# A feed-forward block on one core: ScalarE seeds the accumulation banks, and one more pair is computed by seven quarter products

## Chip, core and metric

The kernel runs on one core of a Trainium2 chip. The metric is device time in microseconds; the median of three runs is compared. Engines: PE is TensorE's matmul, PEld its weight load, DVE is VectorE, ACT is ScalarE, POOL is GpSimd, SP is SyncE, which here issues the weight DMAs.

## The reference

One residual block on x with 512 rows and 1024 columns, in float32:

```python
def _swiglu(x, w_in, w_out):
    gate, up = jnp.split(x @ w_in, 2, axis=-1)
    return (jax.nn.silu(gate) * up) @ w_out

h = x
h = h + 0.5 * _swiglu(_rmsnorm(h, ffn1_norm), ffn1_w_in, ffn1_w_out)
z = _rmsnorm(h, mix_norm) @ w_in
...                                   # conv module and gated linear attention on z
h = h + jnp.concatenate([y_conv, y_gla], axis=-1) @ w_out
h = h + 0.5 * _swiglu(_rmsnorm(h, ffn2_norm), ffn2_w_in, ffn2_w_out)
gate = jax.nn.sigmoid(_rmsnorm(h, ple_norm) @ ple_w_gate)
h = h + gate * (p @ ple_w_proj)
return _rmsnorm(h, final_norm)
```

The two SwiGLU layers have 2816 hidden columns (`ffn1_w_in` is 1024 x 5632, `ffn1_w_out` 2816 x 1024). "First layer" and "second layer" below are these two.

## The kernel before

**Matmuls in three parts.** Each float32 operand is split into a high part in the matmul's type and a low part (value minus high part). A product is three matmuls: high by high, high by low, low by high (`mm3`, and inside `mul`). For weights, ACT makes the high part (`high`, a cast), DVE the low part (`low`, a subtraction), 128 x 1024 elements at a time. The pools `raw` (fetched weights), `wh` and `wl` (parts) have six buffers each; `sm` (weight sums) has two.

**h.** The residual is kept transposed: eight tiles `hT[0..7]`, 128 columns of the model by 512 rows each.

**A layer** is written by `ffn`. The 22 blocks of 128 hidden columns are 11 pairs. A pair needs gate and up of two blocks, which is a 2 x 2 block product: weights a11, a12 (gate; first and second half of the model's columns) and a21, a22 (up), against the normalised input in four quarters b11, b12, b21, b22.

- *Plain pair:* eight half units h0 to h7 (`plain_unit`), each 12 matmuls on 512 columns. Units h0 to h3 give the gate of the two blocks, h4 to h7 the up; every second unit ends a bank.
- *Pair by seven quarter products* (Winograd's form of Strassen's scheme): units m1, m2, m6, m7, m5, m4, m3 (`mul`), each 24 matmuls on 256 columns, with weight operands a11, a12, s2, s3, s1, a22, s4. The sums s1 to s4 are made by DVE (`s12`, `s3_`, `s4_`, four operations on 128 x 1024), the input sums t1 to t4 once for the layer (`Right.split` makes their parts at given units, the hooks).

In a quarter-product pair, `p.x` is the bank that m1, m6, m5 and m3 add up in, `p.w` that of m7 and m4, `p.y` that of m2. ACT copies `p.x` to SBUF after m1 (`p.a`), m6 (`p.u2`) and m5, and DVE adds the copies to the other banks (`plus`). The first half of the gate is `p.a + p.y`, times the row factor, then silu (`gate0`).

**The output projection** takes the hidden blocks in five cuts, `CUTS = ((0, 4), (4, 8), (8, 12), (12, 16), (16, 22))`. `second` writes a cut as pieces: two of the eight blocks of h each, 24 matmuls on 512 columns in two banks. When a block's sum is complete, DVE does `h = 0.5 * ps + h`. The last cut's pieces are in two halves; the others are one piece each (`begin` and `final` both true).

**Order.** `ffn` lists the units, and each unit has jobs (fetch, weight sums, parts) that are written a given number of units ahead (`AHEAD` is 4). `drive` writes them out: a unit's jobs, then the first of the follow-ups left by the unit before, then the unit, then the other follow-ups. PE, DVE and ACT run exactly in the order written, since `Ordered` chains each one's instructions. SP's DMAs and POOL's instructions aren't chained. A tile takes any free buffer of its pool, and what first writes it waits for that buffer's last reader. PSUM has seven banks for these (`bank`).

In both layers, pair 0 is made before `ffn`, pairs 1 and 2 are plain (`plain` is `(1, 2)`) and pairs 3 to 10 by quarter products. From there an iteration i is m6, m7, m5 of pair i, m1 and m2 of pair i+1, a piece of an earlier cut, m4 and m3 of pair i, and another piece. In the last iteration pieces of the last cut stand in the gaps and after it. In the first layer, m4 of pair 10 also starts loading and splitting weights of the next stage (`ahead`).

Of the kernel before, what the change touches and what calls it, by code (L numbers as in the profile page):

```python
# [62 lines left out]
def block_kernel(ctx: ExitStack, tc: tile.TileContext, a: dict, out: bass.AP):  # L63
# [32 lines left out]
    def bank():  # L96
        return pp.tile([P, SEQ], F32, tag="mm", bufs=7, name=nm("ps"))
# [108 lines left out]

        return low(high(r3))

    def mm3(ps, wh, wl, xh, xl, first, last):
        pe.matmul(ps, wh, xh, start=first, stop=False)  # L210
        pe.matmul(ps, wh, xl, start=False, stop=False)
        pe.matmul(ps, wl, xh, start=False, stop=last)

    def ahead(src, c0, ncol):

# [71 lines left out]
    class Norm:  # L287
# [5 lines left out]
        def add(self, h):  # L293
            if self.n == 0:
                act.activation(self.acc, h, AF.Square)
            else:
                sq = tmp("sq", bufs=3)
                act.activation(sq, h, AF.Square)
                self.engine.tensor_tensor(out=self.acc, in0=self.acc, in1=sq, op=ALU.add)
            self.n += 1  # L300
# [8 lines left out]
    def mul(ps, w, x, first, last, ks=range(4)):  # L309

        (wh, wl), k0 = w, ks[0]
        for k in ks:
            xh, xl = x[k]
            for i in range(2):
                cs = slice(i * P, (i + 1) * P)
                o = ps[:, i * HALF:(i + 1) * HALF]
                end = last and k == ks[-1] and i == 1
                pe.matmul(o, wh[:, k - k0, cs], xh, start=(first and k == ks[0] and i == 0), stop=False, skip_group_check=True)
                pe.matmul(o, wh[:, k - k0, cs], xl, start=False, stop=False, skip_group_check=True)
                pe.matmul(o, wl[:, k - k0, cs], xh, start=False, stop=end, skip_group_check=True)  # L320
# [200 lines left out]
    mid = []  # L521
# [73 lines left out]
    def ffn(w_in, w_out, x, gname, given, first, rsb, hooks, plain):  # L595
# [17 lines left out]
        def silu(g):  # L613
            s = tmp("s")
            act.activation(s, g, AF.Silu)
            return s

        def plus(ps, t, i, name):
            o = tmp(name)
            dve.tensor_tensor(out=o, in0=ps, in1=t, op=ALU.add)  # L620
            dve.tensor_tensor(out=two(o), in0=two(o), in1=row(i), op=ALU.mult)
            return o

        def scaled(ps, name):
            o = tmp(name)
            dve.tensor_tensor(out=o, in0=ps, in1=got['rsb'], op=ALU.mult)
            return o
# [6 lines left out]
        def snap(ps, name, **kw):  # L634
            o = tmp(name, **kw)
            act.copy(o, ps)
            return o
# [11 lines left out]
        def m1(p):  # L649
            p.x = bank()  # L650
            mul(p.x, p.part("a11"), x.op["b11"], True, False)
            p.a = snap(p.x, "sq", bufs=3)

        def m2(p):
            p.y = bank()
            mul(p.y, p.part("a12"), x.op["b21"], True, True)

            def gate0():
                p.s0 = silu(plus(p.y, p.a, 0, "g1"))

            return [gate0]

        def m6(p):
            mul(p.x, p.part("s2"), x.op["t2"], False, False)
# [19 lines left out]
        def plain_unit(j):  # L684

            up, i, k = j // 4, j // 2 % 2, j % 2
            def run(p):
                if not j:
                    p.g, p.s = {}, {}
                if not k:  # L690
                    p.x = bank()
                ps = p.x
                wh, wl = p.part(f"a{1 + up}{1 + k}")
                cs = slice(i * P, (i + 1) * P)
                for c in range(4):
                    mm3(ps, wh[:, c, cs], wl[:, c, cs], *x.rows[4 * k + c], k == c == 0, k == 1 and c == 3)
                if not k:
                    return []
                if not up:
                    def gate():  # L700
                        p.s[i] = silu(scaled(ps, "g1"))
                    return [gate]
                return [lambda: gated_block(p, p.s[i], scaled(ps, "u1"), i),
                        lambda: act_parts(p) if i else None]
            return run
# [29 lines left out]
        def second(cut):  # L735

            f0, f1 = cut
            last = f1 == CUTS[-1][1]
            kn = f1 - f0
            nk = kn // 2 if last else kn  # L740
            ps = {}

            def piece(n, g, begin, final, key=None):

                def get():
                    got[f0, n, g] = load(w_out, f0 + g * nk, nk, n * P, 2 * P)

                def make():
                    got[f0, n, g] = parts(got[f0, n, g])

                def run():
                    left = []
                    wh, wl = got.pop((f0, n, g))
                    for i in range(2):
                        if begin:
                            ps[n + i] = bank()
                        cs = slice(i * P, (i + 1) * P)
                        for kk in range(nk):
                            k = g * nk + kk
                            f = f0 + k  # L760
                            mm3(ps[n + i], wh[:, kk, cs], wl[:, kk, cs], *pairs[f // 2].acts[f % 2],
                                k == 0, k == kn - 1)
                        if final:
                            h = hT[n + i]
                            dve.scalar_tensor_tensor(out=h, in0=ps[n + i], scalar=0.5, in1=h,
                                                     op0=ALU.mult, op1=ALU.add)
                            if last:
                                hi = bt(F32R, "hgH")
                                act.activation(hi, h, AF.Copy, scale=vec(gname, n + i))
                                left.append((h, hi, vec(gname, n + i)))  # L770
                    if key:
                        hooks.get(key, lambda *_: None)()
                    if not left:
                        return []

                    def lower():
                        for h, hi, g in left:
                            lo = bt(F32R, "hgL")
                            dve.scalar_tensor_tensor(out=lo, in0=h, scalar=g, in1=hi.bitcast(F32),
                                                     op0=ALU.mult, op1=ALU.subtract)  # L780
                            nhg.append((hi, lo))

                    lower()
                    for h, *_ in left:
                        norm.add(h)

                return [(7, get), (AHEAD, make)], run

            if not last:
                return [piece(n, 0, True, True, ("g2", f0) if n == 0 else None) for n in range(0, DC, 2)]  # L790
            return ([piece(n, 0, True, False) for n in range(0, 6, 2)],
                    [piece(n, 1, False, True) for n in range(0, 6, 2)] + [piece(6, 0, True, False),
                                                                           piece(6, 1, False, True)])

        units, had = [], set()

        def add(kind, i):
            if 0 <= i < npair and (kind, i) not in had:
                had.add((kind, i))
                units.append(unit(kind, i))  # L800
# [4 lines left out]
        for i in plain:  # L805
# [4 lines left out]
                    due = due[1:]  # L810
            if i in cut_of:
                due += second(cut_of[i])
        for unit_ in (("m1", start), ("m2", start), ("m1", start + 1)):
            add(*unit_)
        for i in range(start, npair):
            add("m6", i)
            add("m7", i)
            add("m5", i)
            if i == end:
                half, rest = second(cut_of[i])  # L820
                units.append(half[0])
            else:
                add("m1", i + 1)
            add("m2", i + 1)
            units += due[:1]
            add("m4", i)
            add("m3", i)
            units += due[1:2]
            due = due[2:]
            if i in cut_of and i < end:  # L830
                due += second(cut_of[i])
# [18 lines left out]
    def sums_hooks(x, names, at):  # L850

        h = {}
        for name, key in zip(names, at):
            h[key] = lambda *_, name=name: x.split(name)
        return h
# [569 lines left out]
    u1_ = plain_block(w0, 1, 1)  # L1425
    steps[3]()
    steps[4]()
    hooks = sums_hooks(xb, ("t2", "t3", "t1", "t4"), (("h7", 1), ("h2", 2), ("h5", 2), ("m1", 3)))
    hooks.update({("m7", 10): lambda *_: turn_p(0), ("m5", 10): lambda *_: turn_p(1)})
    hg, norm = ffn(ffn2_in, a["ffn2_w_out"][0], xb, "ple_norm", wf, ((g0, u0), (g1_, u1_)), lambda: mid[1], hooks, (1, 2))  # L1430
    in_order(False)
    pool.on = False
    rs = None
# [95 lines left out]
```

## Time and profile before

| | us |
|---|---|
| median of three runs | 965.26 |
| lowest and highest | 964.85, 966.62 |
| span of the profiled execution | 964.1 |
| first layer, quarter-product part and its end | 95 to 364 |
| mixer and its projections | 364 to 547 |
| second layer, plain part (pairs 0 to 2) | 547 to 631 |
| second layer, quarter-product part and its end | 631 to 897 |
| last gate, projection and norm | 897 to 964 |

The span runs from the first to the last instruction of one profiled execution. Its own time isn't told apart from the three runs; the median is 1.2 us above the span. Almost all instructions carry one line number, that of a recording helper (L46), so groups are told by tile names: `ps` is a bank; `wr`, `wh`, `wl` are fetched weights and their parts; `sm` weight sums; `hgH`, `hgL` parts of the normalised input; `t1H` and so on parts of its sums; `actH`, `actL` parts of the hidden blocks; `g` and `s` a gate before and after silu; `u` and `u2` the up side; `m` their product; `sq` a snapshot of a bank; `h` the residual; `wa` weights of the next stage.

In a group's row stand the engine, the operation, out<-in, the shapes and the count; after the bar its busy time in us, the mean of one in ns, and the idle time of the engine ahead of it with what ended it. In a row of waits stand total, number and longest. A row of the timeline starts with start and duration in us. In a row of windows stand the stretch, its length, and busy time and count of each engine.

### The profile page before, as it was taken

How to read it: one execution, taken by the hardware profiler on the slowest of the kernel's cores; microseconds unless marked ns; L12 is line 12 of the kernel's file. 1: busy time of each engine (PE TensorE's matmuls, PEld its weight loads, DVE VectorE, ACT ScalarE, POOL GpSimd, SP SyncE). 2: the span in 40 equal slices, each digit the busy share in tenths (PEclk: the TensorE clock that was granted, in tenths of full speed). 3: DMA queues.
4: the chain of work that ended last, by engine and by line, in shares of the span. 5: the costliest groups of instructions: out<-in, count | busy, mean ns of one | idle time of the engine just before them, and what ended most of it. 6: DMA issues, size and time to landing. Idle time of an engine off the chain costs nothing.

```text
span 964.1 us, 14124 instructions
## 1 busy us (share of the span) xinstructions
PE 949.9 (99%) x5737; PEld 837.3 (87%) x5737; DVE 736.7 (76%) x983; ACT 435.1 (45%) x661; POOL 39.7 (4%) x49
## 2 busy tenths in 40 slices
PE   8999999999999999999999999999999999999996
PEld 7888999999999978788877888899999999998885
DVE  4877787878788585999986676678978778867554
ACT  4753444344433453463564644354434434345442
POOL 0000000000000410001120000000000000000000
PEclk9999999999999999999999999999999999999999
DMA  8432323243223561125543234123343233334102
GB/s 250 142 117 67 106 74 124 92 132 102 74 88 119 145 173 48 41 85 134 132 100 99 79 96 129 46 67 113 105 132 109 68 106 113 109 110 153 45 1 88
DMA packets 102853, 99.14 MB, mean 103 GB/s; under 512 B 4499, under 2 KB 95717, under 8 KB 102788
## 3 DMA queue, kind: packets, MB, share of 16 engines
q1 hardware_dynamic: 100916, 94.05, 31.6%
q0 software_dynamic: 1296, 3.67, 2.2%
q8 instruction: 45, 0.74, 0.3%
q10 hardware_dynamic: 576, 0.52, 0.2%
q14 instruction: 20, 0.16, 0.1%
HBM read 92.46 MB, written 2.10 MB: 98 GB/s over the span
## 4 chain that ended last, share of the span: by engine, by line
PE 95%; DMA 1%; DVE 1%; ACT 1%; issue 1%; POOL 0%; SPq 0%; POOLq 0%; DVEq 0%; ACTq 0%
PE ps L46 94%; PE ax L46 1%; DMA wr<-in_w_in 1%; DMA x<-in_x 0%; DVE wl L46 0%; ACT wh L46 0%; POOL wa L46 0%; ACT wa L46 0%; DVE g L46 0%; ACT yc L46 0%; DVE ygL L46 0%; DVE actL L46 0%; DVE yc L46 0%; ACT ygH L46 0%; POOLq L1525 0%
## 5 line engine op out<-in xcount | busy, mean ns | idle before, releaser
L46 DVE TENSOR_TENSOR wl<-wr,wh 128x1024 fp32r<-128x1024 f32 (+2 forms) x180 | 213.2, 1196 | 53.5 <-ACT wh L46 53.3
L46 PE MATMUL ps<-hgH,wh 128*128 128x256 f32 (+1 forms) x768 | 243.3, 322 | 0.0
L46 PE MATMUL ps<-hgH,wl 128*128 128x256 f32 (+1 forms) x768 | 241.7, 320 | 0.0
L46 PE MATMUL ps<-hgL,wh 128*128 128x256 f32 (+1 forms) x768 | 241.1, 319 | 0.0
L46 ACT CAST wh<-wr 128x1024 fp32r<-128x1024 f32 (+2 forms) x185 | 186.2, 1022 | 57.9 <-PE ps L46 38.1
L46 PEld LDWEIGHTS ps<-hgH,wh 128*128 128x128 f32 x768 | 146.3, 191 | 13.0 <-ACT hgH L46 2.0
L46 PEld LDWEIGHTS ps<-hgL,wh 128*128 128x128 f32 x768 | 146.6, 191 | 10.7
L46 PEld LDWEIGHTS ps<-hgH,wl 128*128 128x128 f32 x768 | 145.9, 191 | 9.6
L46 PE MATMUL ps<-actH,wh 128*128 128x512 f32 x352 | 138.4, 393 | 1.3 <-ACT actH L46 1.3
L46 PE MATMUL ps<-actL,wh 128*128 128x512 f32 x352 | 138.1, 392 | 0.2 <-DVE actL L46 0.2
L46 PE MATMUL ps<-actH,wl 128*128 128x512 f32 x352 | 137.8, 391 | 0.0
L46 ACT ACTIVATE s<-g 128x512 f32<-128x512 f32 x48 | 30.4, 633 | 186.3 <-DVE g L46 186.2
L46 DVE SCALAR_TENSOR_TENSOR cv<-glu,cw,cv 128x504 f32<-128x504 f32 (+25 forms) x120 | 81.3, 731 | 0.6
L46 PEld LDWEIGHTS ps<-actH,wh 128*128 128x128 f32 x352 | 66.6, 189 | 14.7 <-ACT actH L46 1.7
L46 PEld LDWEIGHTS ps<-actH,wl 128*128 128x128 f32 x352 | 66.5, 189 | 14.1
L46 PEld LDWEIGHTS ps<-actL,wh 128*128 128x128 f32 x352 | 66.7, 189 | 13.2 <-DVE actL L46 0.5
L46 DVE SCALAR_TENSOR_TENSOR h<-ps,h 128x512 f32<-128x512 f32 x80 | 54.1, 687 | 30.8 <-PE ps L46 30.8
L46 PE MATMUL ps<-wh,hgH 128*128 128x512 f32 (+1 forms) x136 | 52.4, 385 | 0.0
L46 PE MATMUL ps<-wl,hgH 128*128 128x512 f32 (+1 forms) x136 | 51.8, 381 | 0.0
L46 PE MATMUL ps<-wh,hgL 128*128 128x512 f32 (+1 forms) x136 | 51.3, 377 | 0.0
L46 ACT COPY sq<-ps 128x512 f32<-128x512 f32 x32 | 18.7, 585 | 67.3 <-PE ps L46 67.3
L46 ACT CAST actH<-m 128x512 fp32r<-128x512 f32 x44 | 25.7, 618 | 46.1 <-DVE m L46 46.1
(226 smaller groups left out, 1564.7 us busy)
## 6 DMA issues: line engine op xcount, KB each, us to landing
wr<-in_ffn_w_in SPq DMA_DIRECT2D x84, 512.0 KB
wr<-in_ffn_w_out SPq DMA_DIRECT2D x32, 512.0 KB
wr<-in_w_in SPq DMA_DIRECT2D x20, 512.0 KB
wr<-in_ffn_w_out SPq DMA_DIRECT2D x16, 384.0 KB
wr<-in_w_out SPq DMA_DIRECT2D x8, 512.0 KB
wr<-in_ple_w_gate SPq DMA_DIRECT2D x8, 512.0 KB
wl<-wr POOLq DMA_DIRECT2D x5, 512.0 KB, 5.6
x<-in_x SPq DMA_DIRECT2D x8, 256.0 KB
```

Source lines behind the costliest of these rows:

```text
L46: inst = call(*args, **kwargs)
```

## The change

- For the first four cuts, ACT writes 2h into the two banks of a piece two units ahead of it (`seed`); the matmuls add to that without a start flag, and ACT writes 0.5 times the bank back to h. DVE's operation on h goes there. The last cut is as before.
- After m1, ACT copies `p.x` into a new bank `p.y` in place of an SBUF tile; m2 adds to it, and the gate is that bank times the row factor.
- The silu of a gate is written as a second follow-up, behind the next unit's matmuls.
- m1 of pair i+1 stands ahead of m5 of pair i; at the start m1 of the first two pairs stands ahead of m2.
- In the second layer pair 2 is made by quarter products (`plain` is `(1,)`), and the parts of the input sums are made earlier.

```diff
-    def mm3(ps, wh, wl, xh, xl, first, last):
+    def mm3(ps, wh, wl, xh, xl, first, last, skip=False):
...
         def m1(p):
             p.x = bank()
             mul(p.x, p.part("a11"), x.op["b11"], True, False)
-            p.a = snap(p.x, "sq", bufs=3)
+            p.y = bank()
+            act.copy(p.y, p.x)

         def m2(p):
-            p.y = bank()
-            mul(p.y, p.part("a12"), x.op["b21"], True, True)
+            mul(p.y, p.part("a12"), x.op["b21"], False, True)

             def gate0():
-                p.s0 = silu(plus(p.y, p.a, 0, "g1"))
-
-            return [gate0]
+                p.g0 = times_row(p.y, 0, "g1")
+
+            def gate1():
+                p.s0 = silu(p.g0)
+
+            return [gate0, gate1]
...
                 if not up:
                     def gate():
-                        p.s[i] = silu(scaled(ps, "g1"))
-                    return [gate]
+                        p.g[i] = scaled(ps, "g1")
+
+                    def gate1():
+                        p.s[i] = silu(p.g[i])
+
+                    return [gate, gate1]
...
+                onto = begin and final
+
+                def seed():
+                    for i in range(2):
+                        ps[n + i] = bank()
+                        act.activation(ps[n + i], hT[n + i], AF.Copy, scale=2.0)
...
-                        if begin:
+                        if begin and not onto:
                             ps[n + i] = bank()
...
                             mm3(ps[n + i], wh[:, kk, cs], wl[:, kk, cs], *pairs[f // 2].acts[f % 2],
-                                k == 0, k == kn - 1)
-                        if final:
+                                k == 0 and not onto, k == kn - 1, onto)
+                        if onto:
+                            act.activation(hT[n + i], ps[n + i], AF.Copy, scale=0.5)
+                        elif final:
...
-                return [(7, get), (AHEAD, make)], run
+                return [(7, get), (AHEAD, make)] + ([(2, seed)] if onto else []), run
...
-        for unit_ in (("m1", start), ("m2", start), ("m1", start + 1)):
+        for unit_ in (("m1", start), ("m1", start + 1), ("m2", start)):
             add(*unit_)
         for i in range(start, npair):
             add("m6", i)
             add("m7", i)
+            add("m1", i + 1)
             add("m5", i)
             if i == end:
                 half, rest = second(cut_of[i])
                 units.append(half[0])
-            else:
-                add("m1", i + 1)
             add("m2", i + 1)
...
-    hooks = sums_hooks(xb, ("t2", "t3", "t1", "t4"), (("h7", 1), ("h2", 2), ("h5", 2), ("m1", 3)))
+    hooks = sums_hooks(xb, ("t2", "t3", "t1", "t4"), (("h5", 1), ("h7", 1), ("m1", 2), ("m1", 3)))
...
-    hg, norm = ffn(ffn2_in, a["ffn2_w_out"][0], xb, "ple_norm", wf, ((g0, u0), (g1_, u1_)), lambda: mid[1], hooks, (1, 2))
+    hg, norm = ffn(ffn2_in, a["ffn2_w_out"][0], xb, "ple_norm", wf, ((g0, u0), (g1_, u1_)), lambda: mid[1], hooks, (1,))
```

More of the change, by code (lines that the diff above doesn't have):

```diff
@@ L207, in parts @@
         return low(high(r3))
-    def mm3(ps, wh, wl, xh, xl, first, last):
-        pe.matmul(ps, wh, xh, start=first, stop=False)
-        pe.matmul(ps, wh, xl, start=False, stop=False)
-        pe.matmul(ps, wl, xh, start=False, stop=last)
+    def mm3(ps, wh, wl, xh, xl, first, last, skip=False):
+        pe.matmul(ps, wh, xh, start=first, stop=False, skip_group_check=skip)
+        pe.matmul(ps, wh, xl, start=False, stop=False, skip_group_check=skip)
+        pe.matmul(ps, wl, xh, start=False, stop=last, skip_group_check=skip)
     def ahead(src, c0, ncol):
```

## Prediction

> **What bounds the kernel now.** I read the page's busy lines and chain first, then the windows of the stage that the change touches, then TensorE's timeline, then the waits.
>
> ```profile
> span 964.1 us, 14124 instructions
> ...
> PE 949.9 (99%) x5737; PEld 837.3 (87%) x5737; DVE 736.7 (76%) x983; ACT 435.1 (45%) x661; POOL 39.7 (4%) x49
> ...
> PE 95%; DMA 1%; DVE 1%; ACT 1%; issue 1%; POOL 0%; SPq 0%; POOLq 0%; DVEq 0%; ACTq 0%
> ```
> ```profile
> core 0: us, PE busy (x) PEld busy (x) DVE busy (x) ACT busy (x) POOL busy (x), PEclk, DMA share, GB/s
> 571.21:592.97 21.76, 21.76 (x98) 18.02 (x97) 16.06 (x21) 9.11 (x13) 0.00 (x0) 1.00 0.38 120
> 592.97:631.05 38.08, 38.08 (x170) 31.55 (x168) 25.36 (x30) 13.94 (x18) 0.00 (x0) 1.00 0.27 82
> 662.42:693.50 31.08, 31.08 (x218) 29.18 (x217) 25.25 (x30) 13.41 (x17) 0.00 (x0) 1.00 0.33 102
> ```
>
> The windows are the second layer's second pair (eight half units), its third pair (eight half units and three output pieces), and one later iteration (seven quarter products and two pieces). PE is busy for the whole of each, at clock 1.00. DVE and ACT have idle time in all of them. So what a layer costs is the sum of its matmuls' issue intervals; helpers count only where they make PE wait. The intervals, from first rows of four groups:
>
> ```profile
> 592.97 0.39 PE L46 MATMUL ps<-hgH,wh 128*128 128x512 f32 x1
> 603.85 0.39 PE L46 MATMUL ps<-actH,wh 128*128 128x512 f32 x1
> 631.05 0.28 PE L46 MATMUL ps<-hgH,wh 128*128 128x256 f32 x1
> 651.20 0.40 PE L46 MATMUL ps<-actH,wh 128*128 128x512 f32 x1
> ```
>
> Rows one and two enclose four half units of 12 matmuls, 48 in 10.88 us: 0.2267 us per 512 columns. Rows three and four enclose seven products of 24, 168 in 20.15 us: 0.1199 us per 256 columns, 2.88 us per product. Half units take 2.72 us, pieces 5.44. Two halves cost more than a whole: the line through both has 13.1 ns per matmul and 0.417 ns per column.
>
> **The change, part by part.**
>
> *Third pair of the second layer.* Eight half units go: 96 x 0.2267 = 21.76 us. Seven products come: 168 x 0.1199 = 20.15 us. PE gains 1.61 us. All of it is on the path, as the 38.08 row shows. This is the only term on PE. The Trainium skill, "TensorE: Matmul & The Clock Gate", section "Wait — 56ns, not 53.3ns?", puts the warm fixed cost at about 2.5 ns per matmul; by its N / 2.4 GHz plus 2.5 ns the pair would save 96 x 215.8 - 168 x 109.2 ns = 2.4 us, an estimate. The two rows here disagree with it, and I keep 1.61.
>
> *What it asks of the helpers*, with these prices:
>
> ```profile
> L46 ACT CAST wh<-wr 128x1024 fp32r<-128x1024 f32 x167 | 172.2, 1045 | 52.9 <-PE ps L46 38.1 <-issue 7.8 <-DMA wr<-in_ffn_w_out 5.0
> L46 ACT ACTIVATE s<-g 128x512 f32<-128x512 f32 x48 | 30.4, 633 | 186.3 <-DVE g L46 186.2
> L46 ACT COPY sq<-ps 128x512 f32<-128x512 f32 x32 | 18.7, 585 | 67.3 <-PE ps L46 67.3
> L46 ACT ACTIVATE hgH<-h,vcol 128x512 fp32r<-128x512 f32 x24 | 16.8, 718 | 18.2 <-DVE h L46 18.2
> L46 DVE TENSOR_TENSOR wl<-wr,wh 128x1024 fp32r<-128x1024 f32 x162 | 196.3, 1221 | 45.1 <-ACT wh L46 45.0
> L46 DVE SCALAR_TENSOR_TENSOR h<-ps,h 128x512 f32<-128x512 f32 x80 | 54.1, 687 | 30.8 <-PE ps L46 30.8
> L46 DVE TENSOR_TENSOR g<-ps,sq 128x512 f32<-128x512 f32 x16 | 11.0, 685 | 0.0
> ```
>
> The pair needs seven weight parts instead of four and four weight sums: on DVE 3 + 4 operations of 1.22 us and two more 0.69 us gate operations, 9.9 us; on ACT 3 casts of 1.05 us and three PSUM copies of 0.585 us, 4.9 us. Its weight DMAs stay four of 512 KB, asked for in another order.
>
> *2h by ScalarE.* Four of five cuts have 8 blocks in each layer, so 64 of the 80 `h<-ps,h` operations leave DVE: -44.0 us. ACT takes 64 seeds and 64 final scalings. No row shows ACT writing PSUM. The nearest are 0.585 us (PSUM to SBUF) and 0.718 us (SBUF to SBUF, scale from a column); I take 0.65 us per seed and keep both ends. The Trainium skill, "ScalarE: Activation LUTs", section "What happens when an `exp` ACTIVATE runs", says ScalarE writes PSUM faster than SBUF; no row here can show that. ACT's total grows by 64 x 0.65 + 64 x 0.585 = 79 us, from 45% of the span to 54% with the pair: still no bound.
>
> *First quarter product by ScalarE.* The copy stays a copy, now into the bank of the second product, and one of two DVE additions goes (0.685 us x 16 pairs = -11.0 us). The new wait: m2 needs the copy. One product lies between, 2.88 us; the copy starts about 0.2 us after m1 ends and takes 0.6, so about 2.1 us are spare. The cover for this is the new order (m1 of the next pair ahead of m5); without it PE would wait some 0.8 us in each pair. On ACT the copy stands ahead of a weight cast and two seeds. With m1 go its cast and subtraction, and its weight DMA is asked for one unit sooner. SP's order of DMAs stays the same (a11 still follows the piece and precedes a12), and each waits for a freed buffer anyway. POOL has nothing here (0.00 in the windows).
>
> *Seeds in one iteration.* Call m6's start 0. The units run m6, m7, m1' to 8.64, m5, m2' to 14.40, piece A to 19.84, m4, m3 to 25.60, piece B to 31.04. ACT: copy 8.84 to 9.43, one cast to 10.48, A's seeds at 11.1 and 11.8; A needs the first at 14.40, so 3.3 us are spare. After A: scaling 20.04 to 20.63, silu to 21.26, one cast to 22.31, B's seeds at 23.0 and 23.6; B needs the first at 25.60: 2.6 us spare. Behind each scaling stand silu, cast and seeds; the silu's reader, m4 of the next iteration, is far off. Banks: at A's seeds x and w of this pair, x and y of the next, and A's two are 6 of 7; at B's, 5.
>
> The silu is the weak point, for it also waits for DVE. Where DVE stands in an iteration of before:
>
> ```profile
> 203.71 0.40 PE L46 MATMUL ps<-actH,wh 128*128 128x512 f32 x1
> 207.04 0.69 DVE L46 TENSOR_TENSOR g<-ps,sq 128x512 f32<-128x512 f32 x1
> 207.76 0.69 DVE L46 TENSOR_TENSOR g<-g,bc 128x512 f32<-128x512 f32 x1
> 208.37 0.68 DVE L46 SCALAR_TENSOR_TENSOR h<-ps,h 128x512 f32<-128x512 f32 x1
> 208.48 0.63 ACT L46 ACTIVATE s<-g 128x512 f32<-128x512 f32 x1 [4.77 <-DVE g L46]
> ```
>
> m2' ended at 203.71 and its gate was ready at 208.45, 4.7 us into A. Now the gate is one operation and the silu is asked only after A, 5.44 us in, so the gate is there first, with about 0.7 + 0.7 us over.
>
> *Start of the second layer.* Here cover is thinnest. In the 21.76 us of the second pair DVE works 16.06 us. Drawn into that stretch are two more weight parts, three sums (6.1 us) and a second operand split (1.4 us): 23.6 us, so DVE ends about 2 us late. In the seven products after it DVE has nine operations of 1.22 us, seven of 0.69 and four of half that, 17.2 us in 20.15. The parts are made four units (over 10 us) ahead, so PE doesn't see this; but the third pair's gate comes about 6 us after its product and holds the silu, two casts and A's seeds. Laying the rows end to end, A's first seed is ready 2 us before PE wants it, and so is B's. I count the start at nothing on that cover; each us of further lag beyond 2 costs 1 us once.
>
> **Sum.** 964.1 - 1.6 = 962.5 us of span. The median, 965.26, lies 1.2 us above the span shown; with the same surroundings the forecast is 965.26 - 1.61 = 963.65 us.
>
> **Rivals.**
>
> *Late seeds (slower).* If ACT's writes, or DVE's lag before a silu, use up the spare time, PE stands at a piece. Sixteen second pieces in each layer's iterations lie behind a silu; if each waited x us past its 2.6, the sum is 963.6 + 16x, slower by 0.2% from x = 0.22 and 980 us at x = 1. For it: the silu waits below. Against: PE rows show no wait of that place, and DVE loses 55 us. The start alone, 4 us late, would give 967.6.
>
> ```profile
> ACT s L46 <- DVE g L46: 186.2, 46, 6.7
> ...
> PE ps L46 <- ACT actH L46: 1.3, 1, 1.3
> ```
>
> *The end of the first layer gets shorter (faster).* The one real PE stall of the FFNs stands there:
>
> ```profile
> 340.77 0.39 PE L46 MATMUL ps<-actH,wl 128*128 128x512 f32 x1
> 342.48 0.50 PE L46 MATMUL ps<-actH,wh 128*128 128x512 f32 x1 [1.32 <-ACT actH L46]
> ...
> 347.19 0.39 PE L46 MATMUL ps<-actH,wl 128*128 128x512 f32 x1
> ```
> ```profile
> 332.88 1.15 ACT L46 CAST wa<-wr 128x512 fp32r<-128x512 f32 x2 [2.34 <-DMA wr<-in_w_in]
> 334.56 1.14 ACT L46 CAST wa<-wr 128x512 fp32r<-128x512 f32 x2 [0.53 <-DMA wr<-in_w_in]
> 335.61 0.83 ACT L46 CAST wh<-wr 128x768 fp32r<-128x768 f32 x1
> 338.83 0.63 ACT L46 ACTIVATE s<-g 128x512 f32<-128x512 f32 x1 [2.38 <-DVE g L46]
> ```
>
> 340.77 to 347.19 holds 12 intervals: 6.42 us instead of 2.72, 3.7 us lost. If a lighter DVE removed it, 963.65 - 3.7 = 959.9 us. Against: the silu is late because ACT stood in casts of the next stage's weights that waited for DMAs, and neither these nor the last cut (still on DVE) change. I expect the stall to stay.
>
> *Smaller fixed cost per matmul (faster).* With 0 instead of 13.1 ns the pair saves 1.61 + 72 x 13.1 ns = 2.55 us: 962.7 us. The PE rows speak against it. The clock-gate page of the Trainium skill has the rule that would bring it near this.
>
> **Numbers.** 0.2% is 1.9 us, about what a measurement can tell here from no change; so the forecast falls within it, at 963.2 to 964.1, with chance 0.66, of which 0.09 I count past the lower bound (963.33). End of first layer shorter 0.08, fixed cost 0.03, both faster. Late seeds 0.16: 0.04 too small to matter, 0.12 slower. Anything else 0.07: 0.02 faster, 0.03 same, 0.02 slower. Faster 0.22, same 0.64, slower 0.14. Range 961.9 to 966.6: part of the shorter end, and a start up to 3 us late.
>
> **What would show it.** PE in the second layer without gaps, the third pair's products 20.15 us; `h<-ps,h` x16 on DVE; ACT near 520 us; seeds and copies of 0.58 to 0.72 us; no wait PE <- ACT ps at pieces or m2; the stall near 341 us still 3.7 us. Wrong if PE waits for ACT at piece starts, if ACT's PSUM writes take over 1.5 us, or if the stall near 341 moves by over 0.5 us.

## The result and the profile after

| | before | after |
|---|---|---|
| median of 20 runs, us | 964.5 | 963.18 |
| lowest and highest, us | 963.87, 966.62 | 962.3, 965.88 |
| span of the profiled execution, us | 964.1 | 961.4 |

The ratio after to before is 0.9986, with a 95% interval of 0.998 to 0.9992: 1.35 us less, between 0.8 and 1.9 us. That lies inside the 0.2% that the prediction takes for about no change. It has the sign of the 1.61 us summed there, and its interval holds that size.

The page's busy lines of after, and its chain by engine:

```profile
span 961.4 us, 14302 instructions
...
PE 947.4 (99%) x5809; PEld 838.4 (87%) x5809; DVE 693.6 (72%) x912; ACT 504.4 (52%) x795; POOL 38.8 (4%) x49
...
PE 95%; DMA 1%; DVE 1%; ACT 1%; issue 1%; POOL 0%; SPq 0%; POOLq 0%; DVEq 0%; ACTq 0%
```

DVE gave up 43 us and ACT took 69 us; the chain is PE's as before. The groups that the change made or shrank (busy us, mean ns, idle time ahead):

```profile
L46 ACT ACTIVATE h<-ps 128x512 f32<-128x512 f32 x64 | 38.1, 595 | 115.1 <-PE ps L46 115.1
L46 ACT ACTIVATE ps<-h 128x512 f32<-128x512 f32 x64 | 35.9, 598 | 0.0
L46 DVE SCALAR_TENSOR_TENSOR h<-ps,h 128x512 f32<-128x512 f32 x16 | 10.5, 684 | 4.6 <-PE ps L46 4.6
L46 ACT COPY ps<-ps 128x512 f32<-128x512 f32 x17 | 9.7, 571 | 42.4 <-PE ps L46 42.4
```

A seed took 0.598 us and a copy from bank to bank 0.571. The seeds' idle time is 0.0: ACT never sat waiting for h or for a free bank in front of one. PE's rows around the third pair of the second layer, its first matmul and the first of the piece behind its last product:

```profile
591.56 0.39 PE L46 MATMUL ps<-hgH,wl 128*128 128x512 f32 x1
591.79 0.28 PE L46 MATMUL ps<-hgH,wh 128*128 128x256 f32 x1
...
611.82 0.28 PE L46 MATMUL ps<-hgH,wl 128*128 128x256 f32 x1
611.94 0.40 PE L46 MATMUL ps<-actH,wh 128*128 128x512 f32 x1
```

611.94 - 591.79 = 20.15 us: seven products without a gap, where eight half units took 21.76. The pair began 1.18 us earlier than before (592.97); with the pair's 1.61 us that makes up the 2.7 us between the spans, to within 0.1.

Where do 1.18 us ahead of the pair come from? From the end of the first layer, and not from what the change does. Windows of before and of after just behind the stall near 341 us (busy us of each engine, granted clock, DMA share, GB/s):

```profile
343.60:347.00 3.40, 3.40 (x10) 2.66 (x9) 3.40 (x5) 1.76 (x3) 0.00 (x0) 0.50 1.12 279
```
```profile
344.70:348.00 3.30, 3.30 (x16) 2.72 (x15) 3.30 (x5) 1.36 (x3) 0.00 (x0) 1.00 1.08 283
```

In that execution of before, PE ran at a granted clock of 0.50 for 3.4 us behind the stall, which loses 3.4 x 0.5 = 1.7 us; in that of after at 1.00. A later start of the first layer gives 0.5 us of it back (its first piece begins at 68.19 us, before at 67.66), which leaves the 1.2. So the profiled execution of before was a long one: the 20 runs of after each lie 1.7 us above their own spans, which by that distance puts it near 965.8 us (an estimate), 1.3 above the median of before. The two medians are 1.3 us apart, half of the 2.7 us between the two spans, and the change is read from them.

### The profile page after: what moved, and what is told of

It is laid out like the page before. It is cut to its first block, busy times and chain, and to the rows that moved or that the text cites. A ratio compares the mean times of both kernels' runs of the same rounds, so it can differ in the third digit from the quotient of the medians.

```text
span 961.4 us, 14302 instructions
## 1 busy us (share of the span) xinstructions
PE 947.4 (99%) x5809; PEld 838.4 (87%) x5809; DVE 693.6 (72%) x912; ACT 504.4 (52%) x795; POOL 38.8 (4%) x49
## 4 chain that ended last, share of the span: by engine, by line
PE 95%; DMA 1%; DVE 1%; ACT 1%; issue 1%; POOL 0%; SPq 0%; POOLq 0%; DVEq 0%; ACTq 0%
PE ps L46 94%; PE ax L46 1%; DMA wr<-in_w_in 1%; DMA x<-in_x 0%; DVE wl L46 0%; ACT wh L46 0%; POOL wa L46 0%; ACT wa L46 0%; DVE g L46 0%; ACT yc L46 0%; DVE ygL L46 0%; DVE actL L46 0%; DVE yc L46 0%; ACT ygH L46 0%; POOLq L1540 0%
## 5 line engine op out<-in xcount | busy, mean ns | idle before, releaser
L46 PE MATMUL ps<-hgH,wh 128*128 128x256 f32 (+1 forms) x768 | 239.6, 317 | 0.0
L46 PE MATMUL ps<-hgH,wl 128*128 128x256 f32 (+1 forms) x768 | 238.0, 315 | 0.0
L46 PE MATMUL ps<-hgL,wh 128*128 128x256 f32 (+1 forms) x768 | 237.9, 315 | 0.0
L46 ACT ACTIVATE h<-ps 128x512 f32<-128x512 f32 x64 | 38.1, 595 | 115.1 <-PE ps L46 115.1
L46 ACT ACTIVATE s<-g 128x512 f32<-128x512 f32 x48 | 30.2, 629 | 91.4 <-DVE g L46 91.4
L46 DVE TENSOR_TENSOR actL<-m,actH 128x512 fp32r<-128x512 f32 x44 | 28.7, 689 | 43.1 <-ACT actH L46 42.9
L46 DVE TENSOR_TENSOR wl<-sm,wh 128x1024 fp32r<-128x1024 f32 x34 | 41.4, 1218 | 10.1 <-ACT wh L46 10.1
```

Of the source, the lines that this page charges most:

```text
L46: inst = call(*args, **kwargs)
```

## The experiments

Each kernel is the changed kernel with one edit, unless it says otherwise. Its time stands beside the ratio to the kernel before, timed on the same chip.

**Which part of the change brings the 1.35 us?** Two halves of it.

*The changed kernel with the second layer's third pair plain again:*

```diff
-    hooks = sums_hooks(xb, ("t2", "t3", "t1", "t4"), (("h5", 1), ("h7", 1), ("m1", 2), ("m1", 3)))
+    hooks = sums_hooks(xb, ("t2", "t3", "t1", "t4"), (("h7", 1), ("h2", 2), ("h5", 2), ("m1", 3)))
...
-    hg, norm = ffn(ffn2_in, a["ffn2_w_out"][0], xb, "ple_norm", wf, ((g0, u0), (g1_, u1_)), lambda: mid[1], hooks, (1,))
+    hg, norm = ffn(ffn2_in, a["ffn2_w_out"][0], xb, "ple_norm", wf, ((g0, u0), (g1_, u1_)), lambda: mid[1], hooks, (1, 2))
```

> The changed kernel with the second layer's third pair by eight half units again and the input sums' parts made where they were before; seeds, final scalings, copy, order and gates stay changed. Theory A (PE's issue intervals are the time, and the third pair is the whole gain): PE has the matmuls of before, so 0 us against before, within 0.3 us. Rival B (the gain is DVE's relief, some 55 us of work moved or dropped): faster than before by the 1.3 us of the changed kernel.

Measured 964.4 us, ratio 0.9998 (0.9989 to 1.0007), span 963.0. Seeds, copies and the new order, which take 52 us off DVE (684.9 us busy here), are worth nothing that can be measured. This profiled execution has no half clock near 344 us, as that of after has none, and the two spans are 1.6 us apart (963.0 and 961.4): the pair's 1.61 us.

*The kernel before with only that pair by quarter products* (the same two lines, the other way, in the kernel before):

> The kernel before with the third pair of the second layer by quarter products and the input sums' parts made as early as in the changed kernel; DVE still does the work on h and the two additions. Theory A alone: 1.6 us faster, as for the full change. Theory A with a limit by DVE: laying the rows end to end, DVE falls so far behind at the layer's start that PE waits about 1.6 us once (near m5 of the third pair), which cancels the gain: 0 us, between 1.6 faster and 2 slower, with a PE wait in the trace between 595 and 620 us.

Measured 963.51 us, ratio 0.9991 (0.9982 to 1.0), span 961.8. The stall that was expected is far smaller. PE's rows at m5 of the third pair:

```profile
606.13 0.28 PE L46 MATMUL ps<-t3H,wl 128*128 128x256 f32 x1
606.46 0.39 PE L46 MATMUL ps<-t1H,wh 128*128 128x256 f32 x1
```

0.33 us where 0.12 is the pitch: 0.2 us lost, and 0.1 more in the next interval, not 1.6. DVE stood at 745.6 us, 78%, and still was in time. So the pair hardly needs the relief of DVE that comes with it in this change. The time alone does not show it: its interval reaches from -1.7 to 0 us, and holds both the whole gain and none.

**Does the new order hide the copy?** m1 of the next pair directly ahead of its m2, as before:

```diff
-            add("m1", i + 1)
             add("m5", i)
+            add("m1", i + 1)
```

> The first product of the next pair is put directly ahead of its second again, behind m5, in 13 iterations; all else is as in the changed kernel. Theory (the one product between them is what hides ScalarE's copy): PE waits once in each of the 13 iterations for the copy, about 0.2 us until it starts, 0.57 us for it and some 0.1 us of handover, 0.8 to 0.9 us: +10.4 to +11.7 us, about 974 us, and a new wait PE <- ACT ps of that sum. Rival (the copy is hidden anyway, since the engine can start on the second bank before the copy ends, or other waits take over): no change, 963.2 us.

Measured 975.58 us, ratio 1.0111 (1.0094 to 1.0128): some 12 us more than the changed kernel. The waits on PE, and one place:

```profile
PE ps L46 <- ACT ps L46: 9.2, 13, 0.7
```
```profile
677.37 0.28 PE L46 MATMUL ps<-hgH,wl 128*128 128x256 f32 x1
678.36 0.39 PE L46 MATMUL ps<-hgH,wh 128*128 128x256 f32 x1 [0.71 <-ACT ps L46]
```

13 waits, as counted. The one shown costs 0.99 - 0.12 = 0.87 us of pitch; 13 of these are 11.3 us. The bank-to-bank copy is free only because one product stands between; the prediction's 0.8 us was right.

**How much spare time have the seeds?** In the trace of after the first seed of a piece is done 1.9 us or more before the piece's first matmul, at all 32 pieces. Asked for one unit ahead instead of two:

```diff
-                return [(7, get), (AHEAD, make)] + ([(2, seed)] if onto else []), run
+                return [(7, get), (AHEAD, make)] + ([(1, seed)] if onto else []), run
```

> The seeds 2h are asked for one unit ahead of their piece instead of two; nothing else differs. Theory (the seeds have 2.9 to 3.5 us of spare time, and ScalarE's order, not its load, is what could make them late): at A the seeds then stand behind m5's copy, about 12.3 us into the iteration, done by 13.5, with 0.9 us left; at B behind nothing that ends later than m4's half. So PE waits in hardly any iteration; at the start of the second layer, where ScalarE stands longest, one wait of up to 3.3 us: +0 to +3.5 us, 963 to 966.5 us. Rival (the spare time is just enough because the seeds are so early): a wait of 1 to 3 us at most of the 32 pieces, +30 us or more.

Measured 969.76 us, ratio 1.0053 (1.0034 to 1.0072): 6.6 us more than the changed kernel, nearly twice the upper end of what was expected. PE lost 1.5 us near 68.3, 1.9 near 143.9, 1.1 near 270.2 and 1.5 near 616.9. ACT's timeline at the second of these, and PE's:

```profile
140.82 0.59 ACT L46 COPY sq<-ps 128x512 f32<-128x512 f32 x1 [1.35 <-PE ps L46]
144.32 1.04 ACT L46 CAST wh<-wr 128x1024 fp32r<-128x1024 f32 x1 [2.91 <-DMA wr<-in_ffn_w_out]
145.27 1.11 ACT L46 ACTIVATE ps<-h 128x512 f32<-128x512 f32 x2
```
```profile
145.92 0.50 PE L46 MATMUL ps<-actH,wh 128*128 128x512 f32 x1 [1.72 <-ACT ps L46]
```

ACT was idle for 2.9 us, waiting to cast output weights that had not landed, and the seeds stood behind that cast. It is the same at the last two places (1.57 and 1.98 us of waiting for such weights); at the first the seeds stood behind a cast and a silu that had waited for DVE's gate. The prediction's timetable of an iteration knew no wait for a DMA on ACT. To test that reading, the seeds stay one unit ahead, but go in front of that unit's cast:

```diff
-        for *_, f in sorted(jobs, key=lambda j: (-j[0], j[1])):
+        for *_, f in sorted(jobs, key=lambda j: (j[0] != 1, -j[0], j[1])):
```

> As in e6 the seeds are asked for one unit ahead of their piece, but in that unit ahead of the weight cast instead of behind it. Theory (in e6 PE waited at the four pieces where the seeds stood on ScalarE behind a cast of output weights whose DMA was late, 1.6 to 2.9 us): the waits at 143.9, 270.2 and 616.9 us go, the one at 68.3 shrinks from 1.5 to about 0.6 us, because a silu still stands ahead of it: 963.2 + 0.6 = 963.8 us. Rival (one unit is too near by itself, since the seed then also stands behind m5's copy): the 6.6 us of e6 stay, 969.8 us.

Measured 963.9 us, ratio 0.9994 (0.9986 to 1.0003); 963.8 was expected. The three waits are gone, and the first shrank to this:

```profile
PE ps L46 <- ACT ps L46: 0.4, 1, 0.4
```

*Nothing ahead:* `(0, seed)` in that line of the changed kernel.

> The seeds are asked for at the piece itself (nothing ahead); nothing else differs. Theory (the late-seed case of the prediction becomes real here): at B the seeds stand behind m3's gate and silu, so PE waits for VectorE's gate 0.7, the silu 0.63 and the first seed 0.6 and their handovers, 2 to 4 us at each of some 13 second pieces in the two layers together, and about 0.8 us at each first one: +40 to +80 us, 1005 to 1045 us, with a wait PE <- ACT ps at the first matmul of the pieces. Rival (seeds are never on the path, since ScalarE is idle half the time): no change, 963 us.

Measured 1064.8 us, ratio 1.1043 (1.1017 to 1.1069): 102 us more than the changed kernel, above the upper end. Waits, one second piece (the last matmul ahead of it started at 673.37), DVE and ACT at that place, and windows over most of the two layers:

```profile
PE ps L46 <- ACT ps L46: 63.5, 30, 3.8
```
```profile
677.43 0.80 PE L46 MATMUL ps<-actH,wh 128*128 128x512 f32 x1 [3.79 <-ACT ps L46]
678.02 0.63 PE L46 MATMUL ps<-actL,wh 128*128 128x512 f32 x1
678.45 0.63 PE L46 MATMUL ps<-actH,wl 128*128 128x512 f32 x1
```
```profile
675.54 0.68 DVE L46 TENSOR_TENSOR g<-ps,bc 128x512 f32<-128x512 f32 x1
```
```profile
676.26 0.63 ACT L46 ACTIVATE s<-g 128x512 f32<-128x512 f32 x1 [4.32 <-DVE g L46]
676.79 1.10 ACT L46 ACTIVATE ps<-h 128x512 f32<-128x512 f32 x2
```
```profile
660.00:960.00 300.00, 267.28 (x1707) 243.76 (x1708) 171.58 (x185) 134.30 (x194) 0.00 (x0) 0.94 0.28 85
110.00:340.00 230.00, 206.59 (x1353) 189.58 (x1352) 135.00 (x148) 104.48 (x148) 2.07 (x6) 0.93 0.28 85
```

The waits, 63.5 us, are within the expected 40 to 80. What the expectation left out is the clock: behind such stalls matmuls on 512 columns stood 0.43 us apart instead of 0.227, and the granted clock over the two windows is 0.94 and 0.93. 300 x 0.06 + 230 x 0.07 = 34 us, a little too much, since PE also waited in part of that time; with the waits that is about the 100 us between the spans. 14 of the 30 waits stand at second pieces and are 3.4 to 3.8 us long; three of 2.3 to 2.7 us stand at the first piece of each layer and at the first layer's fifth piece (near 149 us); the other 13, at first pieces, are 0.2 to 0.4 us. That is the late-seed rival of the prediction become real, with 14 second pieces and not the 16 that it counted; the half clock on top of it was not foreseen.

**Is it ACT's load, or its order?** Every seed written twice:

```diff
-                        act.activation(ps[n + i], hT[n + i], AF.Copy, scale=2.0)
+                        for _ in range(2):
+                            act.activation(ps[n + i], hT[n + i], AF.Copy, scale=2.0)
```

> Each seed is written twice, which adds 64 writes of 0.59 us, 38 us, to ScalarE (from 52% to 56% of the span); nothing else differs. Theory (the load of ScalarE is off the path, and the least spare time of the 32 seeds in the trace of the changed kernel is 1.9 us): no PE wait, 963.2 us, within 0.5 us. Rival (what the copy, the scaling and the seeds add to ScalarE already uses up its slack): up to 0.6 us at each of 32 pieces, up to 19 us.

```profile
PE 947.8 (99%) x5809; PEld 838.7 (87%) x5809; DVE 694.5 (72%) x912; ACT 541.6 (56%) x859; POOL 39.1 (4%) x49
```

Measured 963.04 us, ratio 0.9986 (0.9977 to 0.9995), the same as without. 37 us more on ACT cost nothing that can be measured; one late cast in front of a seed cost 1.9 us. It is the order.

**What makes the stall at the end of the first layer?** The prediction put it on ACT's casts of the next stage's weights, which wait for DMAs. Half of them moved behind the first closing piece:

```diff
-                  ("m4", 10): lambda *_: w_ahead.extend([ahead(w_in, D_CONV, 2 * P), ahead(w_in, 0, 2 * P)])})
+                  ("m4", 10): lambda *_: w_ahead.append(ahead(w_in, D_CONV, 2 * P)),
+                  ("g1", 16): lambda *_: w_ahead.append(ahead(w_in, 0, 2 * P))})
```

(The piece got a hook of that name.)

> The changed kernel with half of the next stage's weights (four of the eight casts that wait for DMAs) started after the first closing piece of the first layer rather than at m4 of pair 10. If the stall near 341 us comes from these casts on ACT ahead of the last silu, it goes: 1.5 us of wait plus up to 2.2 us at the low clock after it, so 2 to 3.7 us off the changed kernel's time. If it comes from DVE or from the pieces' own weights, it stays, and the time is the changed kernel's or worse.

The casts in the changed kernel and here, in the same stretch (min, median and max ns; first and last start):

```profile
L46 ACT CAST wa<-wr x8: 615/618/623, 325.9 to 335.5; 128x512 fp32r<-128x512 f32 x8
```
```profile
L46 ACT CAST wa<-wr x8: 604/617/622, 326.1 to 348.7; 128x512 fp32r<-128x512 f32 x8
```

Measured 961.2 us, ratio 0.9964 (0.9951 to 0.9976), span 960.0. PE has no gap near 341 any more, and it is 2.0 us less than the changed kernel: more than the change itself brought.

The path from those casts to PE runs through DVE. DVE's subtraction ahead of the last gate, and that gate, in the changed kernel and here:

```profile
336.88 1.72 DVE L46 TENSOR_TENSOR wl<-wr,wh 128x768 fp32r<-128x768 f32 x1 [2.74 <-ACT wh L46]
338.53 0.68 DVE L46 TENSOR_TENSOR g<-ps,bc 128x512 f32<-128x512 f32 x1
```
```profile
334.62 0.94 DVE L46 TENSOR_TENSOR wl<-wr,wh 128x768 fp32r<-128x768 f32 x1
335.49 0.68 DVE L46 TENSOR_TENSOR g<-ps,bc 128x512 f32<-128x512 f32 x1
```

ACT's cast `wh` stood behind the late casts `wa`, DVE waited 2.74 us for it, and the gate stood behind DVE's subtraction. The edit also moves POOL's subtractions for the same weights. In the changed kernel POOL worked on them from 333.97 to 339.75 us, and DVE's subtraction took 1.72 us; here POOL was idle then, and it took 0.94. So up to 0.8 us of the gate's delay may be POOL's; the run does not separate the two.

**The same pair in the first layer.**

```diff
-    hooks = sums_hooks(xb, ("t2", "t3", "t1", "t4"), (("h5", 1), ("h7", 1), ("h3", 2), ("m1", 3)))
+    hooks = sums_hooks(xb, ("t2", "t3", "t1", "t4"), (("h5", 1), ("h7", 1), ("m1", 2), ("m1", 3)))
...
-                   (ps0[:2], ps0[2:]), lambda: spread(mid[0]), hooks, (1, 2))
+                   (ps0[:2], ps0[2:]), lambda: spread(mid[0]), hooks, (1,))
```

> The changed kernel with the first layer's third pair by quarter products too, its input sums' parts at the same units as in the second layer. Theory A: a further 1.6 us off, 2.9 to 3.2 us against before, less up to 1 us where the first layer's start (which also makes the sums themselves among its half units) lets PE wait. Rival B: no gain beyond the changed kernel's, or a loss, since DVE gets 9.9 us more work.

Measured 962.88 us, ratio 0.9986 (0.9978 to 0.9995): no further gain that can be measured. PE at m5 of that pair, and ACT ahead of it:

```profile
72.91 0.39 PE L46 MATMUL ps<-t1H,wh 128*128 128x256 f32 x1 [1.02 <-ACT u L46]
```
```profile
68.12 0.62 ACT L46 CAST actH<-m 128x512 fp32r<-128x512 f32 x1 [4.67 <-DVE m L46]
68.65 0.58 ACT L46 COPY ps<-ps 128x512 f32<-128x512 f32 x1
69.16 1.32 ACT L46 CAST hgH<-xg 128x256 fp32r<-128x256 f32 x4
70.39 1.99 ACT L46 CAST wh<-wr 128x1024 fp32r<-128x1024 f32 x2
72.28 0.57 ACT L46 COPY u<-ps 128x512 f32<-128x512 f32 x1
```

m6's bank was ready near 69; its copy u was made at 72.28, behind six casts, and m5 writes that bank. Against that, the casts of t4 (`hgH<-xg`) have time: with their hook at `("m6", 2)` in place of `("m1", 3)` they stand behind the copy. Both edits and the moved weights in one kernel:

> Three things on top of the changed kernel: half of the next stage's weights are asked for behind the first closing piece (as in e4), the first layer's third pair goes by quarter products (as in e3), and that pair's fourth operand split stands behind m6's copy instead of behind m1 of the next pair. Theory (in e3 the saved 1.6 us were given back because m6's copy u stood on ScalarE behind four operand casts and two weight casts): without that wait the pair gives its 1.6 us here too, 961.2 - 1.6 = 959.6 us, ratio to before 0.995. Rival (what held the copy in e3 was VectorE's lateness, through the cast of m that stands ahead of both): PE still waits about 1 us at m5 of the first layer's third pair, 960.7 us or more.

```profile
69.25 1.99 ACT L46 CAST wh<-wr 128x1024 fp32r<-128x1024 f32 x2
71.14 0.58 ACT L46 COPY u<-ps 128x512 f32<-128x512 f32 x1
71.62 1.33 ACT L46 CAST hgH<-xg 128x256 fp32r<-128x256 f32 x4
```

Measured 959.32 us, ratio 0.9944 (0.993 to 0.9958), span 958.3; 959.6 was expected. m5 follows m7 at the usual pitch (71.82 behind 71.70). It beats both kernels: 5.1 us less than before, 3.9 less than the changed kernel.

## Why the prediction was right, step by step

*The only term on PE* was 1.61 us, and the products took the forecast 20.15 us. The runs agree: none of the gain without the pair, 1.35 us with it. By the estimate from the Trainium skill ("TensorE: Matmul & The Clock Gate", section "Wait — 56ns, not 53.3ns?") the pair would have given 2.4 us; the trace, with the same pitches after as before, disagrees with it. The forecast of 963.65 us is 0.5 too high, and most of that is its start: the median of three runs, 965.26, lies 0.8 us above that of 20.

*DVE and ACT.* DVE lost 43 us where 45 were forecast. ACT ended at 504 us, where 520 had been forecast: the seeds were taken at 0.65 us and took 0.598, and seeds and scalings were busy for 74 us instead of 79. Most of the rest is that the sum added single durations, while instructions in a row overlap on ACT: two seeds of 0.598 us take 1.11 us together. The page "ScalarE: Activation LUTs" of the Trainium skill (section "Step-by-step: what each stage is for", which follows the one named in the prediction) says that ScalarE writes PSUM faster than SBUF. The copies from a bank agree, by little: 571 ns into a bank, 585 ns into SBUF before. So does the seed's 598 ns against the 629 ns of the silu, from SBUF to SBUF, though the two operations differ:

```profile
L46 ACT ACTIVATE s<-g 128x512 f32<-128x512 f32 x48 | 30.2, 629 | 91.4 <-DVE g L46 91.4
```

*The timetable of an iteration* held at the points that it named. The copy had the forecast 2.1 us; the seeds 3.5 and 2.9 us, where 3.3 and 2.6 were forecast. It missed four pieces where 1.9 to 2.2 us were left. A wait on ACT for a DMA was not in it, and the run with the seeds one unit ahead shows what that omission can cost. That no seed stands behind such a wait at two units was not worked out; there the prediction was lucky. The waits of after show the same lateness on DVE, off the path (before: 9.6 us, 4 times):

```profile
DVE sm L46 <- DMA wr<-in_ffn_w_in: 36.0, 15, 3.1
```

A DVE with less to do reaches the weights sooner than they land: the wait is 38.3 us in the run with the third pair plain again, and 8.1 in the one with the pair alone. ACT's wait for a gate, which had spoken for late seeds with 186.2 us, is halved (91.4 us, in the silu's row above).

*The start of the second layer* had more cover than was counted. The rows:

```profile
604.76 0.68 DVE L46 TENSOR_TENSOR g<-ps,bc 128x512 f32<-128x512 f32 x1
```
```profile
605.48 0.63 ACT L46 ACTIVATE s<-g 128x512 f32<-128x512 f32 x1 [1.39 <-DVE g L46]
606.01 1.99 ACT L46 CAST wh<-wr 128x1024 fp32r<-128x1024 f32 x2
607.90 1.11 ACT L46 ACTIVATE ps<-h 128x512 f32<-128x512 f32 x2
```

m2 ended at 600.42 by the products' 2.88 us, and the gate was ready 5.0 us later, not 6. A's first seed was done at 608.5, 3.4 us before A at 611.94; 2 had been counted.

*The rivals.* Late seeds did not come, because they stand in front of the casts that wait; the load did not decide it, as the doubled seeds show. The stall at the end of the first layer stayed, as forecast. Its cause is the one given, the casts of the next stage's weights, as the run with half of the weights moved shows; but the path was misread. The silu's row in the prediction shows it waiting 2.38 us for DVE's gate, with ACT idle, and it is DVE that waited for ACT's cast. PE's rows after:

```profile
341.29 0.39 PE L46 MATMUL ps<-actH,wl 128*128 128x512 f32 x1
342.89 0.50 PE L46 MATMUL ps<-actH,wh 128*128 128x512 f32 x1 [1.21 <-ACT actH L46]
343.62 0.50 PE L46 MATMUL ps<-actL,wh 128*128 128x512 f32 x1 [0.23 <-DVE actL L46]
343.96 0.39 PE L46 MATMUL ps<-actH,wl 128*128 128x512 f32 x1
```

Its size was overstated: the 3.7 us read from 340.77 to 347.19 in before held 1.7 us of half clock, which belongs to that execution. Of the kernel's own it is 2.0 us, both in these rows (1.60 + 0.73 + 0.34 us for three pitches of 0.2267) and in the run that removed it. So the prediction's sign that it would be wrong, a stall that moves by over 0.5 us, did come, from 3.7 to 2.0 us. It is not the change that moved it: PE's wait there is 1.2 to 1.3 us before, after, and in either half of the change.

## What to carry to other kernels

Price a step on the bounding engine by its measured pitch; work moved between two engines that both have idle time is worth nothing by itself, however much it is (52 us here). For the helper that takes it over, the order of its queue mattered here and not its load, up to 56% of the span: ask what stands ahead of each new instruction, and whether that waits for a DMA. A short producer, such as the copy or the seed, belongs one product or more ahead of its reader and in front of any cast whose data may be late.

## What was not expected of the hardware

After the same stall of about 2 us, one profiled execution had a window at half clock and another none. The stretch that holds the stall, in before and in after:

```profile
340.20:343.60 3.40, 1.85 (x8) 0.99 (x7) 2.70 (x4) 1.79 (x4) 0.00 (x0) 1.00 0.91 245
```
```profile
341.20:344.57 3.37, 1.94 (x8) 1.07 (x7) 2.69 (x5) 2.35 (x4) 0.00 (x0) 1.00 1.06 289
```

The clock recorded in the traces changes only on a grid. With nothing ahead, the 16 half-clock stretches last 3.4 or 6.8 us each and start whole multiples of 3.413 us apart (677.44, 714.99, 752.54 us and so on, 11 x 3.413 from one to the next). Against the span's start the grid lies differently in each execution: the first change to full clock is at 9.1 us in before, 10.1 in after and 8.4 with nothing ahead. The page "TensorE: Matmul & The Clock Gate" of the Trainium skill (section "What's actually happening") calls the clock's window 3.4 us long and free-running; the traces agree. The rows above are the grid's windows around the stall, and only that of before was followed by the half clock.

That page of the Trainium skill also asks for a whole idle window before the clock falls. The row of before disagrees, for PE was busy for 1.85 of 3.40 us in the window ahead of the fall. How little work makes the clock fall can be estimated. Counting each matmul's columns at the 0.417 ns worked out in the prediction, each of the 17 windows ahead of a fall (one in before, 16 with nothing ahead) holds at most 1.28 us of work, that of before 1.23. That of after holds 1.35, and no window without a fall behind it holds less than 1.16, in any trace from the first full clock to 15 us before the end. That puts the border near 1.2 us of 3.4, between two executions that differ by 0.1 us here. No run was made to test it.
